# One flow-matching block with 32 experts on one core: three groups of 128-column products per expert put together into one

## The chip, the cores and the metric

The kernel runs on one core of one Trainium2 chip. The metric is the device time of one execution in microseconds (us). A profile is one execution recorded by the hardware profiler. The engines are PE (TensorE, matrix products; PEld is its weight load), DVE (VectorE), ACT (ScalarE), POOL (GpSimd) and SP (SyncE, which here only issues transfers).

## The reference, cut to what matters

The block has a first half (input projection, three token mixers, merge, layer norm) and a mixture of 32 experts over 256 latent tokens. Each token goes to its four best experts. The change touches the experts alone:

```python
def expert(acc, xs):
    wgu, bgu, wd, bd, cw = xs
    gate, up = jnp.split(h @ wgu + bgu, 2, axis=-1)      # h 256x1024, wgu 1024x2048
    gate = jnp.minimum(gate, SWIGLU_LIMIT)
    up = jnp.clip(up, -SWIGLU_LIMIT, SWIGLU_LIMIT)
    glu = gate * jax.nn.sigmoid(SWIGLU_ALPHA * gate)
    y = ((up + 1) * glu) @ wd + bd                        # wd 1024x1024
    return acc + cw[:, None] * y, None
```

All is float32. The weights of one expert are 12.58 MB (six pieces of 2 MiB: four of gate/up, two of down), 403 MB for all.

## The kernel before, in words

The first 310 us compute the first half of the block and the routing. Then comes a loop over the 32 experts (`for e in range(NE)`, line 1478 on). An expert takes at most 64 tokens in its usual pass (SLOTS = 64). Where more tokens chose it, a branch on each engine (`tc.If(tv > SLOTS)`, two in each expert, lines 1503 and 1518) runs a second pass over the same weights: `rest_gate` and `rest`.

The steps of one expert, by the names of the helpers:

- `gate_up` (L1392): the gate/up product in two halves of 512 output columns, each over 8 blocks of the inner dimension. A product has 64 stationary columns and 512 moving columns, and two of them, on the two halves of the array's columns, run beside each other. An f32 product is recorded as two instructions, so one half is 32 instructions and a range of four blocks 16. The first half goes to PSUM bank `g0`, the second to `g1`.
- `biases` (L1386): one product with 128 stationary columns that opens a bank with the bias.
- `act` (L1397 to L1401): the clamped SwiGLU of one half, four DVE instructions and a sigmoid on ACT.
- `turn` (L1406, L1407): transposes the result of one half on PE into a scratch bank; ACT copies it to `gT`, the stationary operand of the down product.
- `spots` (L1375 to L1380): two DVE products of the selection with the router's weights, two transposes on PE, and two DVE readings of the scratch bank.
- `select` (L1359, DVE) and `gather` (L1367 on PE, four evacuations L1370 on ACT): the one-hot selection of a pair of experts' tokens, and the tokens themselves. `select` of a pair runs in every even expert, for two experts ahead, and each `gather` makes half of that pair's tokens: the first half in the even expert, right after the `select`, the second in the odd one.
- `bias_of` (L1383, DVE): the stationary operand of the next expert's `biases`.
- `down` (L1414): the down product, 64 stationary columns again, 32 instructions in all.
- `spread` (L1417 to L1419) and `scatter` (L1426): the weighted result, and eight products with 64 rows of the array that add it to the accumulator banks `acc`. `scatter` of one expert runs in the next.

The order of the instructions on every engine is the order of the text (`tc.manual_schedule()`); each engine works its own list off in order and waits for others by semaphores. PSUM has eight banks: four for `acc`, two for `gbank` (`g0` and `g1`, which swap their roles from one expert to the next, since `down` writes into `g0`), and two scratch banks that `sps2()` hands out in turn:

```python
    def sps2():
        sbank.append(sbank.pop(0))
        return sbank[-1]
```

SP issues the weight pieces in the order of use. There are nine places for them. `done(key)` gives a place back and issues the next piece of the queue into it; that issue waits until PE has read the old piece. So the order of `done` calls in the text is the order of the transfers.

Of the kernel before, what the change touches and what calls it, by code (L numbers as in the profile page):

```python
# [24 lines left out]
NE = 32  # L25
SLOTS = 64
# [91 lines left out]
def kernel(ctx, tc, x, cx, cols, rows, csts, wsm, wgt, bada, brt, sgub, bdn, bgu,  # L118
# [29 lines left out]
    def pump():  # L148
        while queue:
            if queue[0][0][0] == "cx":  # L150
                key, src = queue.pop(0)
                nc.sync.dma_start(out=cxt[:, key[1], :], in_=src)
                continue
            for sp in spaces:
                s = sp.slot(2 if queue[0][0][0] in ("gu", "dn") else 1)
                if s is not None:
                    break
            else:
                return
            key, src = queue.pop(0)  # L160
            nc.sync.dma_start(out=s, in_=src)
            loaded[key] = (s, sp, sp.used[-1])

    def weight(key):
        if key not in loaded:
            pump()
        return loaded[key][0]

    def done(key):
        _, sp, rng = loaded.pop(key)  # L170
        sp.free(rng)
        pump()

    def halves(*key):

        w = weight(key)
        return [w[:, 0:2048], w[:, 2048:4096]]
# [47 lines left out]
    with ExitStack() as p1:  # L225
# [848 lines left out]
        for c4 in range(4):  # L1074
# [3 lines left out]
            for br, (k0, k1) in ((0, (0, 2)), (2, (6, 8)), (1, (2, 6))):  # L1078
                ps = zps()
                for b in range(2):  # L1080
                    sl = slice(P * b, P * b + P)
# [238 lines left out]
    gbank = [bank[7], bank[5]]  # L1320
    sbank = [bank[3], bank[4]]
# [4 lines that stand above are left out]
# [19 lines left out]
    def chunk():  # L1345
        return dict(sT=Buf(R, 256), cwv=Buf(A2, 2), gT=Buf(A2, KB, SLOTS), gc=[Buf(A2, 256)])

    yhx, ylx = Buf(R, 512), Buf(R, 512)
    cur, over = chunk(), chunk()
# [23 lines left out]
    def spots(b, sl, e):  # L1373
        for t in range(2):
            V.tensor_scalar_mul(sw[:, t], sl[:, t, :].unsqueeze(1).to_broadcast([P, 2, SLOTS]), cw[:, t, e:e + 1])  # L1375
        pw = sps2()
        for t in range(2):
            T.transpose(pw[:, P * t:P * t + P], sw[:, t].rearrange("p a n -> p (a n)"), ident[:])  # L1378
        V.tensor_scalar(out=b["sT"][:], in0=pw[:, 0:256], scalar1=0.0, scalar2=None, op0=ALU.is_gt)  # L1379
        V.reduce_sum(out=b["cwv"][:, 0:1], in_=pw[:, 0:256], axis=AX.X)  # L1380
# [4 lines left out]
    def biases(e, hf, pg):  # L1385
        mm(pg[:], bse[e % 2][:], bst[:, hf, :], start=True, stop=False, skip_group_check=True)  # L1386

    def gate_up(hT, pg, ks, w):
        for k in ks:
            wk = w[k // 2].rearrange("p (k n) -> p k n", k=2)  # L1390
            for q in range(2):
                mm(pg[64 * q:64 * q + 64, :], hT[:, k, :], wk[:, k % 2, 512 * q:512 * q + 512], start=False, stop=k == KB - 1,  # L1392
                   skip_group_check=True)

    def act(b, hf, pg):
        gc = b["gc"][hf]
        V.tensor_scalar_min(gc[:], pg[:, 0:256], LIMIT)  # L1397
        S.activation(out=sg[:], in_=gc[:], func=AF.Sigmoid, scale=SW_ALPHA)  # L1398
        V.tensor_scalar(out=up[:], in0=pg[:, 256:512], scalar1=LIMIT, scalar2=-LIMIT, op0=ALU.min, op1=ALU.max)
        V.tensor_tensor(out=gc[:], in0=gc[:], in1=sg[:], op=ALU.mult)  # L1400
        V.scalar_tensor_tensor(out=gc[:], in0=up[:], scalar=1.0, in1=gc[:], op0=ALU.add, op1=ALU.mult)  # L1401

    def turn(b, hf):
        pt = sps2()
        for j in range(2):
            T.transpose(pt[:, P * j:P * j + P], b["gc"][hf][:, P * j:P * j + P], ident[:])  # L1406
        S.copy(out=b["gT"][:, 4 * hf:4 * hf + 4, :].rearrange("p (q j) n -> p j q n", q=2),  # L1407
               in_=pt[:, 0:256].rearrange("p (j q n) -> p j q n", j=2, q=2))

    def down(b, py, ks, w):  # L1410
        for k in ks:
            wk = w[k // 2].rearrange("p (k n) -> p k n", k=2)
            for q in range(2):
                mm(py[64 * q:64 * q + 64, :], b["gT"][:, k, :], wk[:, k % 2, 512 * q:512 * q + 512], start=k == 0, stop=k == KB - 1)  # L1414
# [14 lines left out]
    def rest_gate(e, w):  # L1429

        gather(over, 0, 1)
        gather(over, 1, 1)
        pg = sps2()
        biases(e, 0, pg)
        gate_up(over["hT"][:, :, 0, :], pg, range(6), w)
        spots(over, over["sl"][:, :, 0, :], e)
        gate_up(over["hT"][:, :, 0, :], pg, range(6, 8), w)
        act(over, 0, pg)
# [29 lines left out]
    biases(0, 0, gbank[0])  # L1468
    V.tensor_copy(out=cnt[:, 0:NE], in_=ps[0:1, 64:64 + NE])
    V.reduce_max(out=cnt[:, NE:NE + 1], in_=ps[0:1, 64:64 + NE], axis=AX.X)  # L1470
    V.tensor_tensor(out=e4[:], in0=m8[:, :, 0:4], in1=m8[:, :, 0:1].to_broadcast([P, 2, 4]), op=ALU.subtract)
    S.activation(out=e4[:], in_=e4[:], func=AF.Exp)
    V.reduce_sum(out=rs1[:], in_=e4[:], axis=AX.X)
# [5 lines left out]
    for e in range(NE):  # L1479
        p = pair[e // 2 % 2]  # L1480
        q_ = pair[(e // 2 + 1) % 2]
        hT = p["hT"][:, :, e % 2, :]
        w = halves("gu", e, 0) + halves("gu", e, 1)
        select(over["sl"][:], 1, 1, e)
        _, (tv,) = nc.values_load_multi_w_load_instructions(cnt[0:1, e:e + 1], engines=engs, min_val=0, max_val=256)
        if e == NE - 1:
            _, (most,) = nc.values_load_multi_w_load_instructions(cnt[0:1, NE:NE + 1], engines=[*engs, ET.SP], min_val=0, max_val=256)
        g0, g1 = gbank if e % 2 == 0 else gbank[::-1]
        gate_up(hT, g0, range(8), w)
        act(cur, 0, g0)  # L1490
        if e:
            scatter(cur)
        if e == NE // 2:
            for hf in range(2):
                sl = slice(64 * hf, 64 * hf + NE)
                V.tensor_tensor(out=bdnt[sl], in0=bdnt[sl], in1=g2q[sl], op=ALU.mult)
        if e == NE - 4:
            for hf in range(2):
                sl = slice(64 * hf, 64 * hf + NE)
                for t in range(2):  # L1500
                    mm(acc[t][hf][:], cwT[sl, P * t:P * t + P], bdnt[sl], start=False, stop=False, skip_group_check=True)
        over["hT"] = q_["hT"][:, 4:8].rearrange("p k (i j) n -> p (k i) j n", j=1)
        with tc.If(tv > SLOTS):  # L1503
            rest_gate(e, w)
        for i in range(2):
            done(("gu", e, i))
        wu = halves("gu", e, 2) + halves("gu", e, 3)
        biases(e, 1, g1)
        gate_up(hT, g1, range(4), wu)
        spots(cur, p["sl"][:, :, e % 2, :], e)  # L1510
        turn(cur, 0)
        gate_up(hT, g1, range(4, 8), wu)
        act(cur, 1, g1)
        if e < NE - 1:
            wd = halves("dn", e, 0) + halves("dn", e, 1)
        else:
            wd = [weight(("dn1", e, i)) for i in range(4)]
        with tc.If(tv > SLOTS):
            rest(e, g1, wu, wd)
        for i in range(2, 4):  # L1520
            done(("gu", e, i))
        if e + 1 < NE:
            bias_of(e + 1)
        if e % 2 == 0 and e + 2 < NE:
            select(q_["sl"][:], 2, 0, e + 2)
        down(cur, g0, range(4), wd)
        for key in [("dn", e, 0)] if e < NE - 1 else [("dn1", e, 0), ("dn1", e, 1)]:
            done(key)
        turn(cur, 1)
        if e + 2 - e % 2 < NE:  # L1530
            gather(q_, e % 2, 2)
        if e + 1 < NE:
            biases(e + 1, 0, g1)
        down(cur, g0, range(4, 8), wd)
        for key in [("dn", e, 1)] if e < NE - 1 else [("dn1", e, 2), ("dn1", e, 3)]:
            done(key)
        if e < NE - 1:
            spread(cur, g0)
        else:
            ylast, lnb = Buf(A, 512), Buf(A, 2, D)  # L1540
            for i in range(2):
                S.dma_start(out=lnb[:, i, :], in_=lnr[2 + i:3 + i, :].to_broadcast([P, D]))
            V.scalar_tensor_tensor(out=ylast[:], in0=g0[:], scalar=cur["cwv"][:, 0:1], in1=g2q[:], op0=ALU.mult, op1=ALU.mult)
            scatter_whole(cur, ylast, True)
        if e == 0:
            for hf in range(2):
                S.dma_start(out=bdnt[64 * hf:64 * hf + NE], in_=bdn[:, 512 * hf:512 * hf + 512])
            ps = sps2()
            for hf in range(2):
                for t in range(2):  # L1550
                    mm(ps[64 * hf:64 * hf + NE, P * t:P * t + P], cw[:, t], ident[:], start=True, stop=True)
                V.tensor_copy(out=cwT[64 * hf:64 * hf + NE], in_=ps[64 * hf:64 * hf + NE, 0:256])
# [128 lines left out]
```

## Time and profile before

| what | value |
|---|---|
| median of 3 runs | 1285.13 us (1280.12 to 1285.91) |
| the profiled execution | 1286.55 us, its span 1284.7 us |
| PE busy | 1189.9 us (93% of the span), 6619 products |
| DVE, ACT, POOL busy | 461.2 us, 284.5 us, 28.3 us |
| transfers | 471.74 MB, mean 367 GB/s |
| mean granted clock of TensorE | 0.984 of full speed |

A row of the timeline names the start, the busy time, the engine, the line, the operation, what it writes and reads, the shape of the tile and how many instructions are merged; in brackets stands how long the engine sat idle before it and what ended that. A product's end is modelled, so the distance from start to start is the safer reading. A row of the windows gives the busy time of each engine in a stretch, the granted clock and what the transfers did.

### The profile page before, as it was taken

The numbers are of one execution on the slowest core, as the hardware profiler recorded it, in microseconds if no ns is written. First come the engines' busy times: TensorE is split into PE (matmuls) and PEld (weight loads), VectorE is DVE, ScalarE is ACT, GpSimd is POOL, SyncE is SP. The second block draws the span as 40 slices with busy tenths as digits, with TensorE's granted clock in tenths as the row PEclk, the third lists the DMA queues.
The fourth block names the chain that finished last, engine by engine and source line by source line (L and its number), as shares of the span: only waits on it lengthen the run. The fifth ranks groups of instructions, "written<-read, shape, count | busy, mean of one in ns | idle before, by whom it ended". The sixth has DMA issues, their size and how long they took to land. (4 is left out here: it accounts for less than half of the span.)

```text
span 1284.7 us, 16504 instructions
## 1 busy us (share of the span) xinstructions
PE 1189.9 (93%) x6619; PEld 611.3 (48%) x6624; DVE 461.2 (36%) x988; ACT 284.5 (22%) x548; POOL 28.3 (2%) x42
## 2 busy tenths in 40 slices
PE   7997999999999999999999999999888999889884
PEld 5897889995333434334433334333333333333321
DVE  6488768796222222222212221222222122212223
ACT  5352745634111111111111111111111111111101
POOL 1000000002000000000000000000000000000000
PEclk9998999998999999999999999999999999999998
DMA  9745648777999999989959999999999999999993
GB/s 389 274 152 204 232 178 296 294 311 297 392 415 427 424 427 427 427 323 429 375 213 387 428 425 427 427 425 427 427 426 426 427 425 427 425 427 426 428 423 149
DMA packets 39470, 471.74 MB, mean 367 GB/s; under 512 B 4529, under 2 KB 4657, under 8 KB 7473
## 3 DMA queue, kind: packets, MB, share of 16 engines
q1 hardware_dynamic: 37008, 463.75, 87.3%
q10 hardware_dynamic: 1696, 4.40, 1.0%
q8 instruction: 89, 1.46, 0.5%
q0 software_dynamic: 640, 1.84, 0.5%
q14 instruction: 37, 0.30, 0.1%
HBM read 468.92 MB, written 1.05 MB: 366 GB/s over the span
## 5 line engine op out<-in xcount | busy, mean ns | idle before, releaser
L1392 PE MATMUL bank<-arena,arena 128*64 128x512 f32 x1808 | 408.8, 596 | 18.3 <-DMA arena<-in_wgu_dram 17.7
L1414 PE MATMUL bank<-arena,arena 128*64 128x512 f32 x1088 | 251.7, 604 | 25.5 <-DMA arena<-in_wdn_dram 17.9
L1392 PEld LDWEIGHTS bank<-arena,arena 128*64 128x64 f32 x1808 | 124.1, 137 | 260.5 <-issue 235.6
L1414 PEld LDWEIGHTS bank<-arena,arena 128*64 128x64 f32 x1088 | 79.3, 138 | 174.8 <-issue 152.7
L246 PE MATMUL bank<-rounded 128*128 128x256 f32 (+1 forms) x1152 | 149.6, 289 | 0.1
L246 PEld LDWEIGHTS bank<-rounded 128*128 128x128 f32 x1152 | 144.0, 195 | 1.8 <-issue 0.6
L1397 DVE TENSOR_SCALAR arena<-bank 128x256 f32<-128x256 f32 x68 | 28.9, 424 | 280.4 <-PE bank L1392 280.4
L1417 DVE SCALAR_TENSOR_TENSOR arena<-bank,arena,g2q 128x512 f32<-128x512 f32 x33 | 24.8, 751 | 271.8 <-PE bank L1414 163.3
L1398 ACT ACTIVATE arena<-arena 128x256 f32<-128x256 f32 x68 | 28.4, 417 | 366.5 <-DVE arena L1397 362.6
L1407 ACT COPY arena<-bank 128x256 f32<-128x256 f32 x68 | 25.3, 372 | 294.4 <-PE bank L1406 294.4
L1392 PE MATMUL bank<-arena 128*64 128x512 f32 x368 | 85.4, 606 | 3.0 <-DMA arena<-in_wgu_dram 2.6
L343 DVE TENSOR_TENSOR rounded<-arena,rounded 128x2048 fp32r<-128x2048 f32 x29 | 66.2, 2284 | 15.1 <-ACT rounded L338 15.1
L1367 PE MATMUL bank<-arena 128*128 128x128 f32 (+1 forms) x576 | 69.9, 275 | 0.7 <-DVE rounded L1383 0.7
L1367 PEld LDWEIGHTS bank<-arena 128*128 128x128 f32 x576 | 66.9, 192 | 1.5 <-ACT arena L1232 0.8
L1370 ACT ACTIVATE arena<-bank,shc 128x128 f32<-128x128 f32 (+1 forms) x144 | 53.3, 450 | 50.7 <-PE bank L1367 50.7
L338 ACT CAST rounded<-arena 128x2048 fp32r<-128x2048 f32 x29 | 55.0, 1898 | 9.2 <-PE bank L246 5.6
L1379 DVE TENSOR_SCALAR rounded<-bank 128x256 fp32r<-128x256 f32 x34 | 14.5, 425 | 117.0 <-PE bank L1378 117.0
L1392 PEld LDWEIGHTS bank<-arena 128*64 128x64 f32 x368 | 25.2, 139 | 53.6 <-issue 45.3
L1418 ACT CAST rounded<-arena 128x512 fp32r<-128x512 f32 x33 | 20.4, 618 | 111.5 <-DVE arena L1417 111.5
L1426 PE MATMUL bank<-rounded 64*128 64x512 f32 x264 | 40.8, 418 | 3.6 <-ACT rounded L1418 3.1
L1426 PEld LDWEIGHTS bank<-rounded 64*128 64x128 f32 x264 | 22.8, 184 | 33.9 <-issue 25.1
L1386 PE MATMUL bank<-rounded 128*128 128x512 f32 x68 | 32.5, 477 | 5.8 <-PEq L1503 3.8
(326 smaller groups left out, 889.5 us busy)
## 6 DMA issues: line engine op xcount, KB each, us to landing
arena<-in_wgu_dram SPq DMA_DIRECT2D x128, 2048.0 KB, 28.7
arena<-in_wdn_dram SPq DMA_DIRECT2D x62, 2048.0 KB, 27.3
arena<-in_win_dram SPq DMA_DIRECT2D x23, 1024.0 KB, 5.3
arena<-in_wada_dram SPq DMA_DIRECT2D x16, 1024.0 KB, 4.9
arena<-in_wad_dram SPq DMA_DIRECT2D x8, 1024.0 KB, 11.1
arena<-in_wbr_dram SPq DMA_DIRECT2D x4, 1024.0 KB, 5.6
arena<-in_wout_dram SPq DMA_DIRECT2D x4, 1024.0 KB, 5.5
arena<-in_wdn_dram SPq DMA_DIRECT2D x4, 1024.0 KB, 33.6
```

What stands on the lines that cost most here:

```text
L246: mm(o, l, r, start=start and n == 0, stop=stop and n == len(todo) - 1)
L338: S.copy(out=wh[:, 0:2048], in_=w)
L343: V.tensor_tensor(out=wl[:, 0:2048], in0=w, in1=wh[:, 0:2048].bitcast(F32), op=ALU.subtract)
L1367: mm(pg[:, w * k:w * k + w], h2[:, t, 512 * a + P * k:512 * a + P * k + P], b["sl"][:, t].rearrange("p i n -> p (i n)"), start=t == 0, sto ...
L1370: S.activation(out=b["hT"][:, 4 * a + k].rearrange("p i n -> p (i n)"), in_=pg[:, w * k:w * k + w], func=AF.Identity, scale=shc[:, 1, 4 * ...
L1386: mm(pg[:], bse[e % 2][:], bst[:, hf, :], start=True, stop=False, skip_group_check=True)
L1392: mm(pg[64 * q:64 * q + 64, :], hT[:, k, :], wk[:, k % 2, 512 * q:512 * q + 512], start=False, stop=k == KB - 1, skip_group_check=True)
L1397: V.tensor_scalar_min(gc[:], pg[:, 0:256], LIMIT)
L1398: S.activation(out=sg[:], in_=gc[:], func=AF.Sigmoid, scale=SW_ALPHA)
L1407: S.copy(out=b["gT"][:, 4 * hf:4 * hf + 4, :].rearrange("p (q j) n -> p j q n", q=2), in_=pt[:, 0:256].rearrange("p (j q n) -> p j q n", j ...
L1414: mm(py[64 * q:64 * q + 64, :], b["gT"][:, k, :], wk[:, k % 2, 512 * q:512 * q + 512], start=k == 0, stop=k == KB - 1)
L1426: mm(acc[t][hf][:], b["sT"][sl, P * t:P * t + P], y_[sl, :], start=False, stop=last and y_ is ylx, skip_group_check=True)
```

## The change

It reorders one expert. After the first half of gate/up comes the first branch and then the whole second half (its `biases` has been done one expert earlier). Behind it stand, in one group, everything with 128 stationary columns or 64 rows: `scatter` of the expert before, the first `turn`, the second branch, `spots`, `gather`, both `biases` of the next expert and the second `turn`. Then the whole `down` runs, into a scratch bank, and the next expert's gate/up follows directly. `g0` and `g1` no longer swap. The work itself is the same.

```diff
@@ -1468,6 +1468,7 @@
     biases(0, 0, gbank[0])
     V.tensor_copy(out=cnt[:, 0:NE], in_=ps[0:1, 64:64 + NE])
     V.reduce_max(out=cnt[:, NE:NE + 1], in_=ps[0:1, 64:64 + NE], axis=AX.X)
+    biases(0, 1, gbank[1])
@@ -1485,9 +1486,21 @@
-        g0, g1 = gbank if e % 2 == 0 else gbank[::-1]
+        g0, g1 = gbank
         gate_up(hT, g0, range(8), w)
         act(cur, 0, g0)
+        over["hT"] = q_["hT"][:, 4:8].rearrange("p k (i j) n -> p (k i) j n", j=1)
+        with tc.If(tv > SLOTS):
+            rest_gate(e, w)
+        for i in range(2):
+            done(("gu", e, i))
+        wu = halves("gu", e, 2) + halves("gu", e, 3)
+        gate_up(hT, g1, range(8), wu)
+        act(cur, 1, g1)
+        if e < NE - 1:
+            wd = halves("dn", e, 0) + halves("dn", e, 1)
+        else:
+            wd = [weight(("dn1", e, i)) for i in range(4)]
         if e:
             scatter(cur)
...
@@ -1499,41 +1512,30 @@
-        over["hT"] = q_["hT"][:, 4:8].rearrange("p k (i j) n -> p (k i) j n", j=1)
-        with tc.If(tv > SLOTS):
-            rest_gate(e, w)
-        for i in range(2):
-            done(("gu", e, i))
-        wu = halves("gu", e, 2) + halves("gu", e, 3)
-        biases(e, 1, g1)
-        gate_up(hT, g1, range(4), wu)
-        spots(cur, p["sl"][:, :, e % 2, :], e)
         turn(cur, 0)
-        gate_up(hT, g1, range(4, 8), wu)
-        act(cur, 1, g1)
-        if e < NE - 1:
-            wd = halves("dn", e, 0) + halves("dn", e, 1)
-        else:
-            wd = [weight(("dn1", e, i)) for i in range(4)]
         with tc.If(tv > SLOTS):
             rest(e, g1, wu, wd)
         for i in range(2, 4):
             done(("gu", e, i))
+        spots(cur, p["sl"][:, :, e % 2, :], e)
         if e + 1 < NE:
             bias_of(e + 1)
         if e % 2 == 0 and e + 2 < NE:
             select(q_["sl"][:], 2, 0, e + 2)
-        down(cur, g0, range(4), wd)
-        for key in [("dn", e, 0)] if e < NE - 1 else [("dn1", e, 0), ("dn1", e, 1)]:
-            done(key)
-        turn(cur, 1)
         if e + 2 - e % 2 < NE:
             gather(q_, e % 2, 2)
         if e + 1 < NE:
-            biases(e + 1, 0, g1)
-        down(cur, g0, range(4, 8), wd)
+            biases(e + 1, 0, g0)
+            biases(e + 1, 1, g1)
+        turn(cur, 1)
+        py = sps2()
+        down(cur, py, range(4), wd)
+        for key in [("dn", e, 0)] if e < NE - 1 else [("dn1", e, 0), ("dn1", e, 1)]:
+            done(key)
+        down(cur, py, range(4, 8), wd)
         for key in [("dn", e, 1)] if e < NE - 1 else [("dn1", e, 2), ("dn1", e, 3)]:
             done(key)
+        g0 = py
```

## Rows read from the trace of the kernel before

**Rows 1.** Windows: busy time by engine, PEclk, DMA share and GB/s

```profile
650.00:700.00 50.00, 47.27 (x227) 18.40 (x225) 10.35 (x25) 7.18 (x17) 0.00 (x0) 0.97 0.76 304
1100.00:1150.00 50.00, 44.03 (x218) 17.02 (x217) 9.98 (x27) 6.36 (x16) 0.00 (x0) 1.00 1.00 426
```

**Rows 2.** Timeline of PE, first products of the experts 12 and 31

```profile
697.46 7.04 PE L1392 MATMUL bank<-arena,arena 128*64 128x512 f32 x32
...
1239.59 3.65 PE L1392 MATMUL bank<-arena 128*64 128x512 f32 x16 [1.14 <-DMA arena<-in_wgu_dram]
```

**Rows 3.** Costliest groups of the page: the first DVE step of act

```profile
L1397 DVE TENSOR_SCALAR arena<-bank 128x256 f32<-128x256 f32 x68 | 28.9, 424 | 280.4 <-PE bank L1392 280.4
```

**Rows 4.** Timeline of PE, all of expert 16 and the start of the next

```profile
802.79 3.60 PE L1392 MATMUL bank<-arena 128*64 128x512 f32 x16
806.23 3.60 PE L1392 MATMUL bank<-arena,arena 128*64 128x512 f32 x16
809.76 1.20 PE L1426 MATMUL bank<-rounded 64*128 64x512 f32 x8
811.13 0.47 PE L1386 MATMUL bank<-rounded 128*128 128x512 f32 x1 [0.17 <-PEq L1503]
811.53 3.65 PE L1392 MATMUL bank<-arena,arena 128*64 128x512 f32 x16
815.12 0.44 PE L1378 MATMUL bank<-ident,arena 128*128 128x128 f32 x2
...
815.71 3.65 PE L1392 MATMUL bank<-arena,arena 128*64 128x512 f32 x16
819.67 3.65 PE L1414 MATMUL bank<-arena,arena 128*64 128x512 f32 x16 [0.31 <-PEq L1518]
...
823.53 1.95 PE L1367 MATMUL bank<-arena 128*128 128x128 f32 x16
825.24 0.48 PE L1386 MATMUL bank<-rounded 128*128 128x512 f32 x1
825.65 3.65 PE L1414 MATMUL bank<-arena,arena 128*64 128x512 f32 x16
829.13 7.04 PE L1392 MATMUL bank<-arena,arena 128*64 128x512 f32 x32
```

**Rows 5.** Timeline of DVE and ACT in the same expert

```profile
809.88 0.42 DVE L1397 TENSOR_SCALAR arena<-bank 128x256 f32<-128x256 f32 x1 [4.47 <-PE bank L1392]
...
811.31 0.42 DVE L1401 SCALAR_TENSOR_TENSOR arena<-arena 128x256 f32<-128x256 f32 x1
...
813.25 0.48 DVE L1375 TENSOR_SCALAR arena<-arena,cwt 128x128 f32<-128x128 f32 x2 [0.22 <-DVEq L1503]
815.67 0.42 DVE L1379 TENSOR_SCALAR rounded<-bank 128x256 fp32r<-128x256 f32 x1 [1.94 <-PE bank L1378]
816.01 0.41 DVE L1380 TENSOR_REDUCE arena<-bank 128x1 f32<-128x256 f32 x1
...
821.40 0.23 DVE L1383 CAST rounded<-arena 128x128 fp32r<-128x128 f32 x1
821.54 0.42 DVE L1359 TENSOR_TENSOR arena<-iota,posq 128x256 f32<-128x256 f32 x1
...
825.52 1.50 ACT L1370 ACTIVATE arena<-bank,shc 128x128 f32<-128x128 f32 x4 [1.42 <-PE bank L1367]
```

**Rows 6.** Timeline of PE, the products behind three long waits

```profile
342.14 0.62 PE L1551 MATMUL bank<-ident,cwt 128*32 128x128 f32 x4 [2.06 <-DVE cwT L1552]
...
991.35 5.25 PE L1414 MATMUL bank<-arena,arena 128*64 128x512 f32 x16 [2.28 <-DMA arena<-in_wdn_dram]
...
1200.08 3.65 PE L1414 MATMUL bank<-arena,arena 128*64 128x512 f32 x16 [2.41 <-DMA arena<-in_wdn_dram]
```

**Rows 7.** Windows around the first two of them, columns as in the first group

```profile
340.00:345.00 5.00, 2.84 (x11) 1.14 (x12) 2.12 (x5) 0.62 (x1) 0.00 (x0) 0.77 1.02 420
990.00:995.00 5.00, 3.65 (x10) 1.29 (x12) 1.41 (x4) 0.05 (x1) 0.00 (x0) 0.66 1.00 426
```

## The prediction

> **What bounds the kernel now.** I read the windows first, then PE's timeline, then DVE's and ACT's beside it. The windows show two regimes. From 1100 to 1150 us the transfers are busy all the time at 426 GB/s while PE does 44.03 us of 50 [rows 1]: an expert's 12.58 MB take 29.5 us there. From 650 to 700 us it is the other way: PE does 47.27 us and the transfers fall to 304 GB/s, because all nine places hold pieces that PE has not read. The reason is that `act` ran 68 times, not 64 [rows 3]: two experts (in the timeline the 7th and the 10th, counted from 0) take the second pass, which costs PE about 30 us more each. Behind them PE is late; it starts expert 12 at 697.46 us and works at its own pace of 26.34 us an expert, which is what expert 16 shows from 802.79 to 829.13 [rows 4], until it has caught up with the transfers and waits for them.
>
> How much PE waits: from expert 12 to expert 31 it takes 1239.59 - 697.46 = 542.1 us [rows 2]; 19 experts at 26.34 are 500.5, and expert 30 has no gather (2 less). So about 43 us of PE's time are waits for pieces, all late. A change to PE's order therefore has two ways to the end. On the **transfer path** the end moves by as much as PE's arrival at expert 12 moves, because from there the transfers run without a break. On the **PE path** it moves by what all 32 experts gain or lose, less 43 us of slack. The later of the two counts. About 0.5% (6.4 us) is what a measurement can tell from no change.
>
> **The change, part by part.** One expert before [rows 4]: 32 instructions of a half take 2 x 3.44 us (806.23 - 802.79), so the three halves are 20.64 of the 26.34 us, and all else 5.7.
>
> *Removed.* The stream of 64-column products is broken by other products at three places now and at one then. A break costs little: 16 instructions take 3.59 us ahead of the transposes (815.12 - 811.53) and 3.48 ahead of products of their own kind (829.13 - 825.65), so 0.1 to 0.15 on the way out, and about 0.2 on the way back (a `biases` is 0.40 us from start to start, 811.13 to 811.53, of which the streaming is about half, an estimate). Two breaks less are worth 0.6 us an expert. The Trainium skill, TensorEngine Tiling (Array Packing), section Tiling Modes, says that a change of tiling mode, not only of the tile, drains the engine; that rule speaks for the change, and the 0.1 to 0.15 us on the way out agree with it.
>
> *First branch.* It moves between two 64-column runs. The second branch stands there now: 3.96 us from 815.71 to 819.67 instead of 3.44. I take 0.52; the bound below is 0.17, the idle time of the branch behind `scatter` [rows 4].
>
> *The group.* I count from T, the first product of `scatter`, which starts 0.15 us after the second half ends.
> - PE: `scatter` 1.2 us, the first `turn` 0.28 (815.12 to 815.71 holds two such pairs), the branch 0.17: ready for the transposes of `spots` at T+1.65.
> - DVE: it does `act` of the second half first, since this stands before. By expert 16 [rows 5], L1397 starts 0.12 after T and L1401 ends at 811.73, T+1.97; its branch 0.22 and L1375 0.48 follow: T+2.67. So the transposes start at T+2.75: PE **waits 1.1 us**. Before, four blocks of gate/up covered this.
> - The transposes end at T+3.03. L1379 starts 0.55 after they began, L1380 ends 1.30 after (816.42 - 815.12): T+4.05. Then `bias_of` 0.14: T+4.2. In even experts `select` 0.42: T+4.6.
> - PE's `gather` reads that `select` in even experts, so it starts at T+4.65, a **wait of 1.6 us**; in odd ones it starts at T+3.03. Before, the first half of `down` (3.44 us) stood between. It takes 1.71 (823.53 to 825.24), the two `biases` 0.44 to 0.82, `turn` 0.28: PE is ready for `down` at T+7.1 (even) and T+5.45 (odd).
> - `down` now writes into a scratch bank. By the turn of `sps2()` (turn, spots, gather, turn, down) it is the one that `gather` used, so it waits for ACT's four evacuations. These start only after the last product of the gather (825.52 - 823.53 = 1.99 behind the first) and take 1.50: with 0.06 for the signal, 3.55 after the gather starts. `down` starts at T+8.2 (even) or T+6.58 (odd), a **wait of 1.1 us**. The trace of before has no such wait; its bounds are 0 and 3.55 less what PE does meanwhile, and I take the upper one because the bank is wholly overwritten. Length of the second `biases` and the old cover of the second `turn` vanish in it. ACT's copy of that `turn` comes behind the evacuations, at T+8.6, four blocks ahead of its use.
>
> The expert is 20.64 + 0.52 + 0.15 + 8.2 = 29.5 us when even, 27.9 when odd; 3.2 and 1.55 more than 26.34, 4.7 a pair.
>
> *Other edits with one answer.* `biases(0, 1)` ahead of the loop waits for a short DVE reading while PE still gathers: nothing. The swap of `g0` and `g1` goes without cost. SP's issues stay in order; those for the last gate/up places come about 1.7 us later, behind `scatter` and `turn`, and those of the first down place in front of one more wait, but up to nine pieces are on their way: nothing. The experts 30 and 31 have no gather; the waits for DVE cost them 3 us together.
>
> *Sum.* Transfer path: six pairs before expert 12 make 28, less 2 because the second pass covers the first wait in two experts: +26. PE path: fifteen pairs 70.6, +3, -2, less 43 of slack: +28. The two agree.
>
> *Clock.* Even experts have 2.7 us of waits with only 0.28 us of transposes in them. After a wait of 2.06 and one of 2.28 us the granted clock fell to its lower level, 1.2 GHz [rows 6, 7], and 16 products took 5.25 instead of 3.65 us; after 2.41 us it did not. If half of 15 even experts lose 1.6 us it is 12, part of it inside the wait for ACT; I take 7. Both ends, 0 and 24, stay for the range.
>
> +28 + 7 = **+35 us** on the profiled 1286.55, which stands 1.4 above the median: 1320 us as a median.
>
> **The rivals.**
> 1. *Faster.* The waits in the group do not appear, and only the breaks count. The group would be 1.2 + 0.28 + 0.17 + 0.28 + 1.71 + 0.44 + 0.28 = 4.4 us and the expert 25.7, 0.6 less; before expert 12 that is 12 x 0.6 = 7 us: 1278. It decides below a group of 5.0 us (26.34 - 20.64 - 0.67). Against it: `act`, `spots` and `select` are one chain on DVE, 4.6 us long. The Trainium skill's rule on mode changes, named above, taken by itself, would have it come out this way.
> 2. *Hidden.* The group is 5 to 5.5 us, and the transfers set the end anyway: 1285. For it stands the 43 us of slack; against it that expert 12 comes before the slack.
> 3. *Half as slow.* `down` does not wait for the evacuations (or `gather` not for `select`): 1.1 us less in each expert, the PE path falls under the slack and the transfer path gives 26 - 13 = +13: 1298.
> 4. *Clock.* It falls in every expert, odd ones too: 30 x 1.6 = 48 on 28: 1361.
>
> **How the numbers follow.** The forecast (+18 to +50) 0.72, rival 1 0.05, rival 2 0.06, rival 3 0.10, rival 4 0.07. Slower is the forecast with rivals 3 and 4: 0.89. The range leaves out rivals 1, 2 and 4 and reaches down to rival 3: 1298, up to the forecast with the upper end of the clock (28 + 24, and 5 for the two `biases` and signals): 1342.
>
> **What would show it.** In the profile after: an expert of some 28.7 us in the stretch from 340 to 500 us, alternating 27.9 and 29.5; before L1378 a wait of 1.1 us for DVE; before L1367 one of 1.6 for L1359 in every second expert; before the first product of L1414 one of 1.1 for ACT L1370; the waits of L1392 and L1414 for transfers (43 us) nearly gone; lower clock behind even groups. Wrong is the prediction if L1414 follows `turn` without a wait, or if PE still waits for pieces for over 20 us.

## The result, and the profile after

The changed kernel takes 1323.68 us (median of 4 runs, 1322.02 to 1323.92) against 1285.27 us: a ratio of 1.0305, with a 95% interval of 1.0284 to 1.0326. It is **slower by 38 us**. The profiled execution took 1322.02 us, 35.5 more than that of the kernel before.

The page of the changed kernel: the busy times by engine, the granted clock, the transfers' share and their rate in 40 slices of the span of 1319.8 us.

```profile
PE 1192.5 (90%) x6619; PEld 644.2 (49%) x6624; DVE 458.7 (35%) x988; ACT 281.7 (21%) x548; POOL 28.4 (2%) x42
...
PEclk9998999998999999999989999989999899999998
DMA  9745568687999999759849999999999999999992
GB/s 391 256 172 200 209 218 310 226 367 303 371 428 428 427 426 426 296 236 400 367 184 366 427 426 426 426 427 426 427 427 427 427 427 427 425 427 426 426 389 78
```

PE is busy almost as long as before (1192.5 us against 1189.9) and idle 32.5 us more. But the sum hides two opposite changes: on the two pages the gather (L1367) takes 90.0 us instead of 69.9, and the long products of L1392 and L1414 together 19.4 us less. So the added time is not waits alone; the slower gather comes up below. Within the loop the transfers pause longest between 500 and 700 us, where the second passes stand, and run without a break afterwards, as before.

The waits of PE in the changed kernel: engine, line, what it waited for, us in total, times, longest.

```profile
PE bank L1378 <- DVE arena L1375: 31.3, 30, 2.3
PE bank L1414 <- ACT arena L1370: 24.7, 30, 0.9
PE bank L1367 <- DVE arena L1359: 21.1, 15, 1.4
```

These three are new, 77 us together. In return none of PE's waits for a piece of the weights is left. In the kernel before they were 38.2 us:

```profile
PE bank L1392 <- DMA arena<-in_wgu_dram: 20.3, 23, 1.8
PE bank L1414 <- DMA arena<-in_wdn_dram: 17.9, 12, 2.4
```

(The 43 us of the prediction come from the starts of the experts [rows 2], so they also hold what PE lost otherwise there, such as the slower products of [rows 6].)

The timeline of PE over expert 2 (even), with the columns of [rows 4]:

```profile
375.51 7.04 PE L1392 MATMUL bank<-arena,arena 128*64 128x512 f32 x32
382.71 3.65 PE L1392 MATMUL bank<-arena,arena 128*64 128x512 f32 x16 [0.16 <-PEq L1493]
386.16 3.63 PE L1392 MATMUL bank<-arena 128*64 128x512 f32 x16
389.73 1.19 PE L1426 MATMUL bank<-rounded 64*128 64x512 f32 x8
390.85 0.44 PE L1406 MATMUL bank<-ident,arena 128*128 128x128 f32 x2
392.25 0.53 PE L1378 MATMUL bank<-ident,arena 128*128 128x128 f32 x2 [0.97 <-DVE arena L1375]
394.19 2.02 PE L1367 MATMUL bank<-arena 128*128 128x128 f32 x16 [1.41 <-DVE arena L1359]
395.97 0.71 PE L1386 MATMUL bank<-rounded 128*128 128x512 f32 x2
396.51 0.38 PE L1406 MATMUL bank<-ident,arena 128*128 128x128 f32 x2
397.81 7.09 PE L1414 MATMUL bank<-arena,arena 128*64 128x512 f32 x32 [0.92 <-ACT arena L1370]
404.73 7.04 PE L1392 MATMUL bank<-arena,arena 128*64 128x512 f32 x32
```

DVE and ACT beside it:

```profile
391.91 0.48 DVE L1375 TENSOR_SCALAR arena<-arena,cwt 128x128 f32<-128x128 f32 x2 [0.22 <-DVEq L1516]
...
393.62 0.42 DVE L1359 TENSOR_TENSOR arena<-iota,posq 128x256 f32<-128x256 f32 x1
396.25 1.51 ACT L1370 ACTIVATE arena<-bank,shc 128x128 f32<-128x128 f32 x4 [4.55 <-PE bank L1367]
397.64 0.39 ACT L1407 COPY arena<-bank 128x256 f32<-128x256 f32 x1
```

Read the brackets against the second fence: PE's transposes (L1378) start when the first of the two L1375 has ended (each takes 0.28 us, so at 392.19), the gather (L1367) when `select` (L1359) has ended, `down` (L1414) when the four evacuations (L1370, 396.25 + 1.51) have ended. The expert takes 404.73 - 375.51 = 29.2 us; the odd ones, without the wait in the middle, take 27.6.

In 11 of the 14 even experts from 2 to 28 the clock fell besides; in the experts 2, 18 and 24 it held, with the same waits. Expert 4 is an example. Its timeline of PE shows the transposes, and the gather, at 3.50 instead of 2.02 us; the window behind it (columns of [rows 1]) shows the granted clock at 0.66 of full speed, a mean of the two levels.

```profile
449.05 0.53 PE L1378 MATMUL bank<-ident,arena 128*128 128x128 f32 x2 [0.97 <-DVE arena L1375]
450.98 3.50 PE L1367 MATMUL bank<-arena 128*128 128x128 f32 x16 [1.41 <-DVE arena L1359]
```

The window from 450 to 455 us:

```profile
450.00:455.00 5.00, 4.02 (x19) 3.87 (x20) 0.84 (x4) 0.47 (x2) 0.00 (x0) 0.66 1.00 426
```

PE's starts of the experts 12 and 31 after the change, to be read against [rows 2]: 28.2 us and 36.8 us later.

```profile
725.66 7.04 PE L1392 MATMUL bank<-arena,arena 128*64 128x512 f32 x32
...
1276.40 3.60 PE L1392 MATMUL bank<-arena 128*64 128x512 f32 x16
```

So 28 us come from the twelve experts up to the end of the second passes, and the rest from PE being the bound from there to the end.

### The profile page after: what moved, and what is told of

Read it like the earlier page. It is cut to its first block, busy times and chain, and to the rows that moved or that the text cites. A ratio compares the mean times of both kernels' runs of the same rounds, so it can differ in the third digit from the quotient of the medians.

```text
span 1319.8 us, 16426 instructions
## 1 busy us (share of the span) xinstructions
PE 1192.5 (90%) x6619; PEld 644.2 (49%) x6624; DVE 458.7 (35%) x988; ACT 281.7 (21%) x548; POOL 28.4 (2%) x42
## 3 DMA queue, kind: packets, MB, share of 16 engines
q0 software_dynamic: 640, 1.84, 0.4%
## 5 line engine op out<-in xcount | busy, mean ns | idle before, releaser
L1392 PE MATMUL bank<-arena,arena 128*64 128x512 f32 x1808 | 401.3, 594 | 5.0 <-PEq L1493 5.0
L1414 PE MATMUL bank<-arena,arena 128*64 128x512 f32 x1088 | 241.9, 596 | 26.3 <-ACT arena L1370 24.7
L1392 PEld LDWEIGHTS bank<-arena,arena 128*64 128x64 f32 x1808 | 137.1, 137 | 260.3 <-issue 258.3
L1414 PEld LDWEIGHTS bank<-arena,arena 128*64 128x64 f32 x1088 | 75.1, 137 | 171.3 <-issue 136.7
L1417 DVE SCALAR_TENSOR_TENSOR arena<-bank,arena,g2q 128x512 f32<-128x512 f32 x33 | 24.8, 751 | 349.4 <-issue 182.8
L1367 PE MATMUL bank<-arena 128*128 128x128 f32 (+1 forms) x576 | 90.0, 323 | 21.8 <-DVE arena L1359 21.1
L1367 PEld LDWEIGHTS bank<-arena 128*128 128x128 f32 x576 | 86.0, 237 | 26.2 <-issue 25.4
L1370 ACT ACTIVATE arena<-bank,shc 128x128 f32<-128x128 f32 (+1 forms) x144 | 53.5, 452 | 141.6 <-PE bank L1367 141.6
L1392 PE MATMUL bank<-arena 128*64 128x512 f32 x368 | 83.3, 593 | 0.1
L1392 PEld LDWEIGHTS bank<-arena 128*64 128x64 f32 x368 | 28.5, 137 | 49.3 <-issue 49.3
L1378 PE MATMUL bank<-ident,arena 128*128 128x128 f32 x68 | 17.9, 333 | 31.3 <-DVE arena L1375 31.3
L1400 DVE TENSOR_TENSOR arena<-arena 128x256 f32<-128x256 f32 x68 | 29.0, 426 | 14.8 <-ACT arena L1398 8.6
L395 DVE SCALAR_TENSOR_TENSOR arena<-arena,sc__144 128x2048 f32<-128x2048 f32 x14 | 32.8, 2342 | 0.0
## 6 DMA issues: line engine op xcount, KB each, us to landing
arena<-in_wdn_dram SPq DMA_DIRECT2D x62, 2048.0 KB, 16.2
```

What stands on the lines that cost most here:

```text
L395: V.scalar_tensor_tensor(out=w, in0=w, scalar=sc_[:, k:k + 1], in1=weight(("ada", g, k - 1)), op0=ALU.mult, op1=ALU.add)
L1367: mm(pg[:, w * k:w * k + w], h2[:, t, 512 * a + P * k:512 * a + P * k + P], b["sl"][:, t].rearrange("p i n -> p (i n)"), start=t == 0, sto ...
L1370: S.activation(out=b["hT"][:, 4 * a + k].rearrange("p i n -> p (i n)"), in_=pg[:, w * k:w * k + w], func=AF.Identity, scale=shc[:, 1, 4 * ...
```

## The experiments

Where a text speaks of the length of an expert, it is the distance from one `spread` (L1417 on DVE) to the next.

### e1: the second turn ahead of the gather

```diff
+        turn(cur, 1)
         if e + 2 - e % 2 < NE:
             gather(q_, e % 2, 2)
         if e + 1 < NE:
             biases(e + 1, 0, g0)
             biases(e + 1, 1, g1)
-        turn(cur, 1)
         py = sps2()
```

> The changed kernel with one edit: the second turn stands ahead of gather, not behind the biases. By the turn of the scratch banks down then writes into the bank that turn used, and no longer into the one that gather used. Theory (three waits for DVE and ACT inside the group make PE late): the wait of down for the evacuations of gather, 24.7 us over 30 experts after the change, goes, and in even experts the turn (0.3 us) falls into the wait for select. PE starts expert 12 about 13 us earlier (6 x 1.2 + 6 x 0.9) than the 725.66 us of the changed kernel, and the transfers behind it set the end: about 1310 us; between 1304 and 1314. Rival (the wait for the bank only hides one that is due anyway, for ACT's copy of the turn or for the weights): the wait of down turns up under another name and the time stays at 1320 to 1325.

Measured: 1307.67 us, ratio 1.0176 (1.0156 to 1.0195). The time is as the theory had it, but not for its reason alone. PE's waits in this kernel:

```profile
PE bank L1378 <- DVE arena L1375: 31.1, 30, 2.3
PE bank L1367 <- DVE arena L1359: 16.2, 15, 1.1
PE bank L1367 <- DVE arena L1380: 9.2, 15, 0.6
PE bank L1392 <- DMA arena<-in_wgu_dram: 6.1, 6, 1.4
```

The wait of `down` is gone, so it was for the bank. But a new one stands in odd experts, third row: the gather now gets the bank that `spots` uses and waits for its readings (L1380). Odd experts therefore take 27.48 us, hardly less than 27.57; only the even ones gain, 27.94 instead of 29.22 where the clock holds. In both halves of the pairs together that was enough to bring the transfers back as the bound (fourth row).

### e2: select at the head of the even expert

```diff
         select(over["sl"][:], 1, 1, e)
+        if e % 2 == 0 and e + 2 < NE:
+            select(q_["sl"][:], 2, 0, e + 2)
...
-        if e % 2 == 0 and e + 2 < NE:
-            select(q_["sl"][:], 2, 0, e + 2)
         if e + 2 - e % 2 < NE:
             gather(q_, e % 2, 2)
```

> The changed kernel with one edit: the select of the next pair stands at the head of the even expert, where DVE has time. Theory: gather no longer waits for select in even experts (21.1 us over 15 experts after the change), and as this was the longest of the waits, the clock falls no more in even experts (12 falls of some 1.4 us). Expert 12 starts about 15 us earlier (6 x 1.4 and five falls), the PE path loses 38 us: about 1308 us. Mean of the products of gather back from 323 to about 275 ns. Rival (the clock falls for another reason than the wait, as the whole group is half empty): the falls stay, only 8.5 us before expert 12 and 21 us in all go: 1305 to 1315 and the mean of the gather products stays above 310 ns.

Measured: 1300.46 us, ratio 1.0127 (1.011 to 1.0144): 23 us of the 38 are back by moving one DVE instruction of 0.42 us. The gather's group on the page shows both effects, no idle time before it and 280 ns a product instead of 323 (line, engine, operation, tile, count, busy time, mean ns of one, idle time before it):

```profile
L1367 PE MATMUL bank<-arena 128*128 128x128 f32 (+1 forms) x576 | 71.9, 280 | 0.0
```

Every expert from 2 to 15 without a second pass takes 27.56 to 27.58 us now. The time lies below the forecast 1308: that counted the 15 us before expert 12 alone. Of the 21.1 us between the profiled executions 16.2 lie before expert 12, and with the transfers as the bound again 4.9 of what PE had lost behind it went as well.

### e3: products of zeros in the waits

```diff
+        if 0 < e < NE - 1:
+            idle2(acc[0][0][:], 3)
         spots(cur, p["sl"][:, :, e % 2, :], e)
+        if e % 2 == 0 and 0 < e < NE - 2:
+            idle2(acc[0][0][:], 5)
```

> The changed kernel with products of zeros put into the group: three ahead of the transposes of spots, five ahead of gather in even experts, each adding nothing to an accumulator bank. They fill 0.65 of the 0.97 us of the first wait and 1.1 of the 1.41 us of the second, so the waits end when they ended. It measures the clock alone. Theory (12 falls of the clock cost 1.4 us each, five of them before expert 12): expert 12 starts 7 us earlier, the PE path loses 17 us: about 1306 to 1314 us, granted clock near 0.98 instead of 0.968. Rival (the falls cost nothing on the path, as they lie within waits for ACT): 1319 to 1325. A third: the products of zeros delay the group by their own 1.7 us: 1340 or more.

Measured: 1311.22 us, ratio 1.0211 (1.0192 to 1.023), granted clock 0.984 in the mean, as in the kernel before. The even experts from 2 to 14 without a second pass take 29.21 to 29.37 us, as expert 2 does in the changed kernel. The waits ended when they ended before, and the gather takes 2.02 us in all 14 even experts, so the clock did not fall there. So the falls cost 12.5 of the 38 us (1323.68 - 1311.22; 7 to 17 by the ends of the two intervals). The three waits are left in e3, and so is the rest of the price; this run does not split it among them.

### e4: e1 and e2 together

> The edits of the last-but-one two together: select at the head of the even expert and the second turn ahead of gather. Theory: of the three waits only the one of the transposes of spots is left (1 us an expert), no clock falls; an expert takes some 26.6 us, 0.3 more than before the change, and expert 12 starts 3 to 5 us later than in the kernel before: 1286 to 1292 us. Rival (something besides the waits and the clock, as the later release of the places or the breaks, makes the change slow): well above, 1300 or more.

(The two edits meant are those of e1 and e2.) Measured: 1303.53 us, ratio 1.0142 (1.0118 to 1.0165). This expectation failed: the two together give no more than e2 alone. The timeline of PE over the end of one expert's group:

```profile
397.29 0.38 PE L1406 MATMUL bank<-ident,arena 128*128 128x128 f32 x2
398.31 2.05 PE L1367 MATMUL bank<-arena 128*128 128x128 f32 x16 [0.63 <-DVE arena L1380]
400.11 0.71 PE L1386 MATMUL bank<-rounded 128*128 128x512 f32 x2
400.76 1.51 PE L1414 MATMUL bank<-arena,arena 128*64 128x512 f32 x6
```

`down` follows without a wait, but the gather waits 0.63 us for the bank of `spots`, and `turn` stands ahead of it. The experts take 27.48 us against 27.57 in e2. What puts e4 above e2 lies ahead of expert 2: its profiled execution is 4.6 us longer and stands 7.2 us behind at the end of expert 1. The clock fell in the gathers of the experts 0 and 1 (3.78 and 2.97 us instead of 1.95) and once between them, and expert 1 took 34.57 us against 31.11. With five uses of two scratch banks in one group, a wait that is taken away at one use turns up at the next.

### e5: everything of DVE done early

e4, and `spots` in two parts:

```diff
         act(cur, 0, g0)
+        weigh(swc, p["sl"][:, :, e % 2, :], e)
+        if e + 1 < NE:
+            bias_of(e + 1)
...
-        spots(cur, p["sl"][:, :, e % 2, :], e)
-        if e + 1 < NE:
-            bias_of(e + 1)
+        spots(cur, p["sl"][:, :, e % 2, :], e, swc, True)
```

`weigh` is the two DVE products of `spots`, into a buffer of its own (`swc`).

> The changed kernel with one group still, but all that DVE does for it done early where that can be: select at the head of the even expert, the two products of spots (into a buffer of their own) and bias_of right behind act of the first half, and the second turn ahead of gather. Theory (DVE's chain inside the group is what makes it long): only a wait of some 0.5 us for the readings of spots is left, as gather uses the bank of spots; an expert takes 26.2 to 26.4 us, as before the change, and the time is 1280 to 1290 us. The breaks saved (0.6 us) are then eaten by that wait. Rival (the reordering has another price, by the branch between two halves or the later release of places): 27 us an expert or more and 1295 us or more.

Measured: 1295.16 us, ratio 1.0085 (1.0071 to 1.01); 27.08 us an expert. The rival's numbers came out. The group:

```profile
388.79 1.22 PE L1431 MATMUL bank<-rounded 64*128 64x512 f32 x8
389.95 0.44 PE L1411 MATMUL bank<-ident,arena 128*128 128x128 f32 x2
390.96 0.41 PE L1383 MATMUL bank<-ident,arena 128*128 128x128 f32 x2 [0.57 <-ACTq L1526]
391.20 0.38 PE L1411 MATMUL bank<-ident,arena 128*128 128x128 f32 x2
392.29 2.05 PE L1368 MATMUL bank<-arena 128*128 128x128 f32 x16 [0.71 <-DVE arena L1385]
```

(Lines are shifted here: L1431 is `scatter`, L1411 `turn`, L1383 the transposes of `spots`, L1368 the gather.) Two waits are left. One is the bank again. The other, 0.57 us, is at the second branch and had been hidden under the wait for L1375: PE goes on 2.17 us after the group began. Whether something that it needs is missing there stays open in this run: the transposes overwrite the bank of the first `turn`, and ACT's copy out of it ends at 390.42 + 0.37 = 390.79, 0.17 us before.

### e6 and e10: two groups

From the changed kernel: the first half of `down` moves up, and the second `turn` and `spots` use the two gate/up banks as scratch.

```diff
-        spots(cur, p["sl"][:, :, e % 2, :], e)
         if e + 1 < NE:
             bias_of(e + 1)
         if e % 2 == 0 and e + 2 < NE:
             select(q_["sl"][:], 2, 0, e + 2)
+        py = sps2()
+        down(cur, py, range(4), wd)
...
+        turn(cur, 1, g0)
+        spots(cur, p["sl"][:, :, e % 2, :], e, g1)
         if e + 2 - e % 2 < NE:
             gather(q_, e % 2, 2)
         if e + 1 < NE:
             biases(e + 1, 0, g0)
             biases(e + 1, 1, g1)
-        turn(cur, 1)
-        py = sps2()
-        down(cur, py, range(4), wd)
```

> Two groups instead of one: scatter, the first turn and the branch between gate/up and the first half of down; the second turn, spots, gather and both biases between the halves of down. bias_of and select stand ahead of the first half of down, whose 3.4 us cover DVE's chain. The second turn and spots use the two gate/up banks as scratch, which are free there, so nothing waits for a scratch bank. Theory (a group costs little by itself, its waits cost): no wait of PE for DVE or ACT is left, an expert takes 25.8 to 26.1 us, 0.3 to 0.5 less than before the change, and the time is 4 to 6 us below that of the kernel before: 1277 to 1282. Rival (PE's lead is lost again, by the place of the branch or new waits for evacuations): equal to before, 1283 to 1288, or slower.

Measured: 1283.57 us, ratio 0.9996 (0.9984 to 1.0008), 26.25 us an expert against 26.34 before the change: no difference that can be measured. All waits for DVE's chain and for the banks are gone, but the branch takes what the saved break gives:

```profile
385.18 0.44 PE L1406 MATMUL bank<-ident,arena 128*128 128x128 f32 x2
386.15 3.65 PE L1414 MATMUL bank<-arena,arena 128*64 128x512 f32 x16 [0.53 <-ACTq L1516]
```

Without that idle time the expert would be 25.72 us; the one before the change without its 0.31 [rows 4] is 26.03. The difference, 0.31 us, is what one break less is worth, less what the first branch costs more in its new place (worked out, not run alone). That a break costs something agrees with the Trainium skill, TensorEngine Tiling (Array Packing), section Tiling Modes, which says that a change of tiling mode drains the engine.

e10 is e6 with `turn(cur, 0)` ahead of `scatter`:

> The kernel in two groups with one more edit: the first turn stands ahead of scatter, so the branch follows the eight products of scatter and not the two short transposes. In the kernel in two groups PE sat idle 0.53 us at that branch; behind scatter, at the other branch of the kernel before, it was 0.17. Theory (how long a branch stops PE depends on how much work is queued ahead of it): the idle time falls to 0.2, an expert takes 25.9 us instead of 26.25, and the time is 1277 to 1282, 3 to 6 us below the kernel before. Rival (the branch takes its half microsecond wherever it stands in the group): 26.2 us an expert and 1282 to 1287.

Measured: 1285.57 us, ratio 1.0015 (1.0001 to 1.003), 26.25 us an expert. The rival held:

```profile
384.33 1.20 PE L1426 MATMUL bank<-rounded 64*128 64x512 f32 x8
386.08 3.65 PE L1414 MATMUL bank<-arena,arena 128*64 128x512 f32 x16 [0.56 <-DVEq L1516]
```

PE goes on 2.12 us after the group's first product, as in e6, whatever stands ahead of the branch. DVE's row of the same stretch shows what that moment is: the last step of `act` ends at 385.50 + 0.43 = 385.93, 0.15 us before PE goes on. In e6 ACT's copy of the `turn` ended at nearly that time too (386.02); here it ends 0.82 us before, so it is not what holds PE.

```profile
385.50 0.43 DVE L1401 SCALAR_TENSOR_TENSOR arena<-arena 128x256 f32<-128x256 f32 x1
```

### e11: without the second branch

e10 without the second branch, and the first with a bound that is never reached.

> The kernel in two groups, turn ahead of scatter, without the second branch and without the second pass (tokens beyond 64 of an expert are left out). In the three kernels e5, e6 and e10 the first product behind the second branch started 0.15 to 0.2 us after DVE's last step of act, whatever stood ahead of the branch. Theory (PE waits at the branch until DVE has passed it, and DVE passes it after act): without the branch, down starts about 1.6 us after the first product of the group instead of 2.1, and an expert takes 25.7 us in the stretch from 360 to 480 us instead of 26.25. Rival (it is down that waits for ACT's copy of the turn or another real dependence): the 0.5 us stay and an expert takes 26.2. The whole time says nothing here, since the transfers set the end without the second pass.

Measured, in one execution (1249.99 us): 25.63 us an expert between 370 and 520 us, and `down` follows `scatter` without a wait, 1.50 us after the group began:

```profile
383.87 0.44 PE L1406 MATMUL bank<-ident,arena 128*128 128x128 f32 x2
384.23 1.21 PE L1426 MATMUL bank<-rounded 64*128 64x512 f32 x8
385.37 3.65 PE L1414 MATMUL bank<-arena,arena 128*64 128x512 f32 x16
```

So `down` needed nothing that was late, and without the branch there is no wait. That PE waits for DVE to come to its own branch is shown best by expert 16 of e10: DVE has 1.39 us more to do ahead of it there, and PE sits idle 1.84 us instead of 0.56, until 0.16 us behind that work. But the branch alone does not do it. In the kernel before, `down` goes on behind the same branch at 819.67 [rows 4], 1.59 us before DVE's last step of `act` ends:

```profile
820.84 0.42 DVE L1401 SCALAR_TENSOR_TENSOR arena<-arena 128x256 f32<-128x256 f32 x1
```

And in e3 the products of zeros behind the branch start while that step still runs, 1.94 us after the group began (their first weight load at 392.71):

```profile
392.55 0.43 DVE L1401 SCALAR_TENSOR_TENSOR arena<-arena 128x256 f32<-128x256 f32 x1
392.95 0.60 PE L1330 MATMUL bank<-zb,identb 128*128 128x512 bf16 x2 [0.36 <-PEq L1516]
```

These write a gate/up bank and an accumulator bank. In e5, e6 and e10 the first product behind the branch writes a scratch bank, and the second pass inside the branch (`rest`) uses the scratch banks too. That this makes the difference fits all five kernels, but no run tests it.

### e7 to e9: no second pass

The bound of both branches is 4 * SLOTS instead of SLOTS, so no second pass runs and the tokens beyond 64 of an expert are left out, in the kernel before (e7), the changed one (e8) and e3 (e9).

> The kernel before without the second pass of the two experts that more than 64 tokens chose (the branches stay, with a bound that is never reached; the tokens beyond 64 of an expert are left out). Theory (PE becomes late only by the second passes, from there the transfers set the end): the stretch with idle transfers between 540 and 690 us goes, some 24 us, and 1258 to 1264 us are left.

> The changed kernel without the second pass of the two experts that more than 64 tokens chose, as in the run before this one. Theory (the waits cost time only as far as PE is late): an expert takes 28.4 us on average with an occasional fall of the clock, the transfers 29.5, so PE waits for pieces through most of the loop and the price of the change shrinks from 38 us to between 0 and 8: 1258 to 1270 us. Rival (each wait of PE costs the end its length, wherever it stands): 35 us above the kernel of the run before, 1295 us or so.

> The changed kernel without the second pass of two experts (tokens beyond 64 of an expert are left out), and with the products of zeros in the group that kept the clock up. Without them this kernel stood at 1265 us, 16 above the kernel before without the second pass, with an expert of 30.5 us when even and 27.6 when odd, together as slow as the transfers. Theory (what is left of the price there is the falls of the clock alone): even experts take 29.2 us, the mean is 28.4, below the 29.4 of the transfers, PE waits for pieces again and the time is 1249 to 1257. Rival (the waits for DVE and ACT cost the end something even where transfers are the limit, as places come free later): 1260 or more.

| kernel | without second pass | with it |
|---|---|---|
| before | 1249.03 us (e7) | 1285.27 us |
| changed | 1265.15 us (e8) | 1323.68 us |
| changed, with products of zeros | 1255.81 us (e9) | 1311.22 us (e3) |

e7 came out 9 us under its range. The idle time of the transfers had been read from the share of busy time; counted in bytes, the stretch from 500 to 700 us (361 of 427 GB/s before the change) holds 31 us of it, not 24. About 5 of the 36 us that went stay open. The windows of the kernel before:

```profile
500.00:700.00 200.00, 193.04 (x954) 76.48 (x952) 45.46 (x113) 28.99 (x74) 0.00 (x0) 0.99 0.88 361
```

and of e7:

```profile
500.00:700.00 200.00, 184.51 (x904) 71.28 (x902) 45.25 (x115) 25.93 (x63) 0.00 (x0) 1.00 1.01 427
```

e8 lies in its range, and the price of the change falls from 38 to 16 us, the way the theory of slack has it. But 0 to 8 us were expected: the time came out because the kernel before it (e7) had been put too high as well. PE doesn't wait for a single piece in e8: the clock fell in 13 of 14 even experts (30.3 us or more), so a pair took nearly as long as its transfers. e9 takes the falls away and 9 of the 16 us with them. About 7 us stay, and the traces place more than half of them: from 300 to 360 us the transfers move 324 GB/s in e9 and 356 in e7, which is 1.9 MB or 4.5 us, and from 360 to 1200 us 427 GB/s in both. So what PE loses in its first experts, before the transfers run without a break, seems not to be covered by the slack.

## Why the prediction was right

The time was forecast at 1320 us, the range 1298 to 1342, and 1323.68 was measured. By its steps:

- **Two paths to the end** held. From the end of `down` of expert 11 to the end of the execution it takes the same time in every kernel in which the transfers are the bound, and more in the changed one, where PE is:

| kernel | L1417 of expert 11 starts | profiled time | difference |
|---|---|---|---|
| before | 697.7 | 1286.55 | 588.9 |
| e6 | 694.5 | 1283.76 | 589.3 |
| e10 | 693.1 | 1282.95 | 589.8 |
| e5 | 704.4 | 1294.19 | 589.8 |
| e2 | 709.8 | 1300.91 | 591.1 |
| e4 | 714.7 | 1305.55 | 590.9 |
| e1 | 722.2 | 1311.81 | 589.6 |
| e3 | 721.7 | 1311.21 | 589.5 |
| changed | 726.0 | 1322.02 | 596.0 |

- **The three waits** were there with the named releasers: 0.97, 1.41 and 0.92 us, forecast at 1.1, 1.6 and 1.1. `down` starts 8.08 us behind the group's first product (forecast 8.2), in odd experts 6.45 (forecast 6.58). The first wait is shorter because the sum let the transposes wait for both L1375; they need only the first (T+2.52, forecast 2.75). Experts of 29.2 and 27.6 us answer to 29.5 and 27.9.
- **The first branch** was priced at 0.52 us and costs 0.32 (382.71 - 375.51 is 7.20 for 32 products of 6.88), with 0.16 us of idle time.
- **The second branch** was taken as 0.17 us, so PE would be ready at T+1.65. For those transposes it is not: e5, where nothing of DVE's chain holds them any more, starts them at T+2.17. In the changed kernel the wait for L1375 hides that, so the sum was not touched, but rival 1, which counted 0.17, was priced too low.
- **The clock** was the term that was mis-sized: 7 us taken, with half of the even experts. It fell in 11 of 14, and e3 measures it at 12.5 us. Without the falls the change costs 27.4 us (1311.22 against the 1283.84 of the same runs), and the forecast without them was 28 by the PE path and 26 by the transfer path, which is the bound in e3. That 1320 lies so near to 1323.68 is in part luck: on the PE path 5.5 us of clock were missing, and a pair of experts became 4.1 us longer (29.2 + 27.6 - 2 x 26.34) where 4.7 were forecast, which over fifteen pairs is 9 us too much.
- **Rival 3** ("1.1 us less in each expert" if one wait is missing) put its finger on the right wait, but e1 shows that taking it away brings 0.1 us in odd experts, as the bank of `spots` is next in line.
- **Breaks**: 0.6 us were forecast for two, and 0.31 for one is what e6 leaves, as far as that sum goes; the gain was too small to count.

## What to carry to other kernels

Before products of one kind are put together, write down what the products in between were covering: here 3.4 us runs of long products hid a chain of DVE steps, and 0.6 us of breaks, by the forecast, were traded for 1.9 us of waits in an odd expert and 3.3 in an even one. A wait for one scratch bank that is taken away comes back at the next use of the same two banks, so count the uses in a group before moving one. And find the stretch in which an engine is late: what it loses before that point the end sees in full, what it loses after it only beyond the slack.

## What the runs showed of the hardware that was not expected

In 11 of 14 even experts the clock fell to its lower level behind two waits of 0.97 and 1.41 us with 0.5 us of transposes between them, so without one long wait; eight products of zeros in these waits (1.85 us of PE's recorded time in expert 2) kept it up in all 14 (e3). And a branch that is not taken can hold PE back with no operand late: 0.56 us in e10, until 0.15 us behind DVE's last step ahead of its own branch, and not at all without the branch (e11). It does not always: in the kernel before PE goes on behind the same branch 1.59 us before that step ends.
